# A conv-and-MLP decoder layer on one core: the gate row turned in DRAM at an earlier product and loaded later, and one quarter's squares run later

## The chip, the core and the metric

The kernel runs on one core of a Trainium2 chip. The metric is the device time of one execution in microseconds (us). A span is the time from the first to the last instruction of one profiled execution. TensorE multiplies (PE in the profile; PEld is its loading of weights), VectorE (DVE) and ScalarE (ACT) do the elementwise work, GpSimd (POOL) does some of it in the first half, and SyncE (SP) issues nearly all transfers, in the order of its program.

## The reference

One layer over 256 tokens of width 2048, in float32: a convolution mixer, then an MLP of width 8192. The last gate is a row of 2048 numbers that scales the MLP's output, column by column.

```python
mod = silu(c) @ mod_w + mod_b
sh1, sc1, g1, sh2, sc2, g2 = split(mod, 6)
h = rms_norm(x, norm1_g) * (1 + sc1) + sh1
x = x + (1 + g1) * conv_mixer(h)
h = rms_norm(x, norm2_g) * (1 + sc2) + sh2
u = square(relu(h @ mlp_w1))             # 256 x 8192
x = x + (1 + g2) * (u @ mlp_w2)          # 256 x 2048
```

## The kernel before

**Tiling.** The MLP's width of 8192 is cut into four quarters (numbered 0 to 3 in the code). A quarter has a first product (`h @ mlp_w1`, called `up`) and a second product (`u @ mlp_w2`, called `down`), which adds to the output `y`, kept in SBUF. Each product is a list of jobs. In quarters 1 to 3 some jobs are Strassen-like block products: the jobs called `seven` in the first product, `eight` in the second. The order of the jobs is written out by hand in two tables, `SEVEN_JOBS` (L75) and `LAST_JOBS` (L78). A number in parentheses there stands for a plain job of the first product, or for an `eight` job of the second. So the second product of a quarter runs `down 4`, `eight 1`, `down 6`, `eight 5`, `eight 7`, `eight 3`, `down 5` and so on.

**Weights.** A weight tile of 1 MB (`raw`, 128x2048) is loaded by SyncE into one of 7 buffers (`top_up`, L212). A job's weights are split in two halves of 128x1024 each: ScalarE writes the rounded part `hi` (L236), VectorE the rest `lo` (L240), each into one of 6 buffers. Three matmuls then take each pair: hi by hi, lo by hi and hi by lo (L310 to L312 in the plain jobs, L376 to L378 in `eight`, L484 to L486 in `seven`). In the block products VectorE first adds one raw tile to another (L336 in `seven`, L356 in `eight`). A buffer of `raw` comes free when the last split or sum that reads it is done, and the next load in SyncE's program may be waiting for it. So TensorE frees `hi` and `lo`, these free `raw`, and this starts loads.

**Activations between the products.** The first product leaves four blocks of 128x512 per token half. A block is transposed by VectorE in squares of 32 (L514), written to a DRAM tile `flat` (L515), and read back in another order (`turn_in`, eight transfers, L532) into two tiles `two`. `square` then runs on ScalarE: relu (L541), square (L543), rounded part (L251), and on VectorE the rest (L254). The results `u2` are the moving side of the second product. `read_block` does the read at once and leaves `square` to a task at the job number that it is given: tasks run while the splits of a job are put out. `block_out` (L1139) calls it for the last two blocks, numbered 2 and 3, from the first job of the second product on, whose number is `at`.

**The gate row.** The columns of `g2` are made by VectorE (L669, then a bias in L624), one per job here and there, as a 128x16 table in `modc`. The last column falls in the third quarter's second product. The table is then written to DRAM as one row of 2048 numbers, 4 bytes at a time (`gates`, L1497), and this row is read back into all 128 partitions as a tile of 1 MB (L1500, into `cond`, called `cb`). `cb` scales the last quarter's results, in `finish` (L446) and in `scale_y` (L1165).

**Order.** A scheduler puts the instructions of each engine in a row by priorities and by its own estimate of time; `issue_after` pins some of them behind others. At run time each engine works through its row in order, and waits on semaphores.

Of the kernel before, what the change touches and what calls it, by code (L numbers as in the profile page):

```python
# [15 lines left out]
P = 128  # L16
T = 256
D = 2048
KT = D // P
FF = 4 * D  # L20
QUARTERS = FF // D
# [57 lines left out]
EIGHT = (1, 2, 3)  # L79
# [8 lines left out]
def conv_block(ctx: ExitStack, tc: tile.TileContext, x, vec, dwq, c_row, mod_r, mod_t, mod_c, w_first, w_in, w_out, w1, w2, out):  # L88
    nc = tc.nc
# [41 lines left out]
    for i in range(2):  # L131
        p = ps.tile([P, 2, 2 * T], F32, name="mm", bufs=2)
        for n in range(2):
            at = 8 * i + 4 * n
            nc.tensor.matmul(p[:, n, :], ones[0:1, :], cond[0:1, at : at + 4, :], start=True, stop=True)
        nc.scalar.activation(cond[:, 8 * i : 8 * i + 8, :].rearrange("p k n -> p (k n)"), p.rearrange("p a b -> p (a b)"), AF.Silu)
    cb = cond.rearrange("p k n -> p (k n)")
    nc.scalar.activation(cz[:, :, 3], col("c", 0, KT), AF.Silu)
    state = {"used": 0}
# [388 lines left out]
    def turn_in(flat):  # L528
        halves = [two() for _ in range(2)]
        for h, s in enumerate(halves):  # L530
            for g in range(4):
                nc.sync.dma_start(  # L532
                    s[32 * g : 32 * g + 32].rearrange("p k (a t) -> p (k a) t", t=32),
                    flat[2 * h : 2 * h + 2, :, :, 32 * g : 32 * g + 32].rearrange("k a i t -> i (k a) t"),
                )
        return halves
# [49 lines left out]
    def mod_tile(at):  # L586
        w = take(("tile", at))
        j = TILES.index(at)
        for k in range(KT):
            g = k % 4  # L590
            state["row_end"] = nc.tensor.matmul(
                row_ps[0][32 * g : 32 * g + 32, j * P : (j + 1) * P], cz[:, k, 0:32], w[:, k, :], start=False, stop=False
            )
# [87 lines left out]
    def mods(keys):  # L681
        for key in keys:
            if key[0] == "mod":
                mod_chunk(*key[1:])
            elif key[0] == "tile":
                mod_tile(key[1])
            else:
                mod_col(key[1])
# [27 lines left out]
    def two():  # L716
        return tmp.tile([P, 2, T], F32, name="two", bufs=6)
# [53 lines left out]
    for job in jobs:  # L771
        n = quota.get(job, 0)
# [5 lines left out]
        if job[:2] in LATE_GATE:  # L778
            n = LATE_GATE[job[:2]][job[2]]
# [132 lines left out]
    for k in range(KT):  # L912
# [4 lines left out]
        if c == 0:  # L917
            n = two()
# [215 lines left out]
    def read_block(at, q, n, flat):  # L1134
        with tc.issue_after(state["load"].ins) if n > 2 else ExitStack():
            halves = turn_in(flat)
        at_job(at, square, q, n, halves)

    def block_out(at, q, n, sums):  # L1139
        flat = new_flat()  # L1140
        for t, _, p in sums:
            turn_out(flat, t, p)
        if n == 3:
            read_block(at + (2 if q in EIGHT else 1), q, 2, kept_of["flats"][0])
            read_block(at + {2: 4, 3: 4}.get(q, 1), q, n, flat)
        else:
            at_job(at + 1, read_block, at + 2, q, n, flat)

# [23 lines left out]
    chain, sums_of, kept_of, half_sums = {}, {}, {}, {}  # L1172
    squared = [None, None]

    for n, job in enumerate(jobs):
# [278 lines left out]
        elif kind == "up":  # L1454
            if job[1:] == (0, 0):
                state["gate_bias"] = x_pool.tile([P, KT], F32, name="gb")
                nc.vector.tensor_copy(state["gate_bias"], col("modb", G2 * KT, KT))
                for k2 in range(HALF):
                    modulate(k2, scaled(k2, r2), SH2, SC2, ps_two())
            if plain:  # L1460
                with urgent():
                    t2 = evac(p)
                    a = two()
                    nc.vector.tensor_tensor(t2, t2, spread(r2), op=ALU.mult)
                    for c in range(2):
                        at = 2 * i + c
                        nc.scalar.activation(t2[:, c, :], t2[:, c, :], AF.Relu, bias=shc[:, at : at + 1])
                    nc.vector.tensor_tensor(a, t2, t2, op=ALU.mult)
                u2[i] = mp.tile([P, 2, 2 * T], F32R, name="u2", bufs=HALF)
                split_act(u2[i], a)  # L1470
            elif i % 2 and job[1] in SEVEN:
                if i == 3 and job[1] in EIGHT[:-1]:
                    room["raw"] -= 1
                at_job(n + 1, block_out, n + 1, job[1], i // 2, sums.pop((kind, i // 2)))
                for k2 in range(2) if i == 7 and job[1] in EIGHT else ():
                    at_job(n + 1, make_half_sums, job[1], k2)
            elif i % 2:
                with urgent():
                    turn_block(job[1], i // 2, sums.pop((kind, i // 2)))
            mods(after[job])  # L1480
            if job[1] == 0:
                if i == 0:
                    turned = scratch.tile([KT, P, T], F32, name="turned")
                    y = xs.rearrange("p k t -> p (k t)").rearrange("p (b f) -> p b f", b=2)
                turn(i)
        else:
            with tc.issue_after(state["w_lo"]), tc.issue_after(state.get("drain", state["w_lo"])):
                mods(after[job])
            if job[1] == 0 and i in SUMS_AT:
                if i == SUMS_AT[0]:  # L1490
                    kept = scratch.tile([4, P, HALF, 2, P], F32, name="kept")
                with tc.issue_after(state["w_lo"]):
                    make_sums(SUMS_AT.index(i))
            if job == ("down", 2, 3):
                gates = scratch.tile([1, D], F32, name="gates")
                with tc.issue_after(state["load"].ins):
                    nc.sync.dma_start(gates[0].rearrange("(k p) -> p k", p=P), modc[:, G2 * KT : G2 * KT + KT])  # L1497
            if job == ("down", 2, 7):
                with tc.issue_after(state["load"].ins):
                    nc.sync.dma_start(cb, gates.to_broadcast([P, D]))  # L1500
            if job == ("down", QUARTERS - 1, 1):
                with tc.issue_after(state["load"].ins):
                    pieces[3] = fetch(3)
            if job == ("down", QUARTERS - 1, 3):
                with tc.issue_after(state["w_lo"]):
                    for t in range(2):
                        at = slice(1536, 2048)
                        scale_y(y[:, t, at], at, pieces[3][t])
            if i % 2 == 0:
                continue  # L1510
            for t, cs, p in sums.pop((kind, i // 2)):
                at = slice(512 * (i // 2) + cs.start, 512 * (i // 2) + cs.stop)
                s = y[:, t, at]
                if job[1] == 0:
                    nc.scalar.activation(s, p, AF.Copy)
                elif job[1] not in EIGHT:
                    state["drain"] = nc.vector.tensor_tensor(s, p, s, op=ALU.add).ins
                else:
                    end = finish if job[1] == QUARTERS - 1 else drain
                    if i in (1, 5):  # L1520
                        at_job(n + 1, end, i // 2, t, cs, p)
                    else:
                        end(i // 2, t, cs, p)
# [59 lines left out]
```

## Time and profile before

| what | value |
|---|---|
| time, median of 3 runs | 1077.24 us (1075.87 to 1087.63) |
| time of the profiled execution | 1076.28 us |
| its span | 1074.5 us |
| PE busy | 1052.1 us, 98% of the span |
| DVE busy | 908.9 us, 85% |
| ACT busy | 607.2 us, 57% |
| mean granted TensorE clock | 0.994 |
| fourth quarter's first product | about 896 to 985 us |
| second quarter's second product | about 643 to 729 us |

The time is 1.78 us above the span; that remainder lies around the first and the last instruction. A busy PE is not by itself a PE at its peak, but in the MLP the matmuls of 128x512 start every 0.23 us and overlap, and a longer step between two starts is time lost. The stage times in the table are read from TensorE's timeline.

### The profile page before, as it was taken

The page shows a single profiled execution, that of the slowest core. Times are in us where ns is not written, and L with a number is a line of the kernel's source. Part 1 is how long each engine was busy: PE and PEld are TensorE (multiplying, and loading weights), DVE is VectorE, ACT ScalarE, POOL GpSimd, SP SyncE. Part 2 cuts the span into 40 slices and gives each one's busy share as a digit, 9 for nine tenths or more (in the row PEclk, how much of TensorE's full clock was granted, in tenths as well). Part 3 has the DMA queues.
Part 4 walks back from the last instruction along what each step waited for, and adds up shares of the span by engine and source line. Part 5 has one row for each costly group of instructions (what it writes and reads, how often), then busy time and mean ns, then how long its engine had stood idle before and what let it go on. Part 6 is the DMA issues. An engine that isn't in the chain of part 4 may idle for free.

```text
span 1074.5 us, 15584 instructions
## 1 busy us (share of the span) xinstructions
PE 1052.1 (98%) x5844; PEld 868.6 (81%) x5844; DVE 908.9 (85%) x1176; ACT 607.2 (57%) x841; POOL 221.4 (21%) x153
## 2 busy tenths in 40 slices
PE   7999999999999999999999999999999999899998
PEld 3888886778699998888888888788888888688886
DVE  5777789988767889877889897999899899599996
ACT  4111298876875687444556576546566645456751
POOL 0000079989599261000000000000000000000001
PEclk8999999999999999999999999999999999999999
DMA  9999997996999978999986997793999792889853
GB/s 384 421 420 420 416 419 306 360 392 238 403 408 403 371 267 294 314 320 323 339 328 225 328 281 242 259 367 124 348 266 288 269 362 86 263 285 348 225 152 59
DMA packets 154334, 331.01 MB, mean 308 GB/s; under 512 B 88465, under 2 KB 114321, under 8 KB 119313
## 3 DMA queue, kind: packets, MB, share of 16 engines
q1 hardware_dynamic: 153248, 328.30, 83.8%
q0 software_dynamic: 864, 1.57, 1.1%
q8 instruction: 46, 0.75, 0.3%
q14 instruction: 30, 0.25, 0.1%
q10 hardware_dynamic: 146, 0.13, 0.0%
HBM read 313.71 MB, written 17.83 MB: 309 GB/s over the span
## 4 chain that ended last, share of the span: by engine, by line
PE 79%; DMA 12%; DVE 5%; ACT 2%; issue 1%; SPq 0%; ACTq 0%; DVEq 0%
PE mm L311 12%; PE mm L312 12%; PE mm L310 12%; DMA raw<-mod_c 9%; PE mm L268 6%; PE mm L269 3%; PE acc L265 3%; PE acc L264 3%; PE acc L266 3%; PE row L576 2%; PE mm L1090 2%; DMA raw<-w 2%; DVE lo L240 2%; PE acc L485 1%; PE acc L486 1%; PE acc L484 1%
## 5 line engine op out<-in xcount | busy, mean ns | idle before, releaser
L236 ACT ACTIVATE hi<-raw 128x1024 fp32r<-128x1024 f32 x374 | 383.4, 1054 | 261.6 <-PE mm L312 122.2
L240 DVE TENSOR_TENSOR lo<-raw,hi 128x1024 fp32r<-128x1024 f32 x313 | 370.6, 1217 | 60.4 <-ACT hi L236 59.9
L240 POOL TENSOR_TENSOR lo<-raw,hi 128x1024 fp32r<-128x1024 f32 x61 | 154.9, 2568 | 29.9 <-ACT hi L236 29.9
L669 DVE SCALAR_TENSOR_TENSOR raw<-raw,cond 128x2048 f32<-128x2048 f32 x50 | 117.7, 2355 | 27.7 <-DMA raw<-mod_c 27.7
L460 POOL DMA_DIRECT2D out<-two x6 | 5.4, 902 | 650.0 <-DVE two L458 638.9
L310 PE MATMUL mm<-hi,u 128*128 128x512 f32 x320 | 124.1, 389 | 0.7 <-ACT hi L236 0.7
L311 PE MATMUL mm<-lo,u 128*128 128x512 f32 x320 | 124.5, 389 | 0.0
L312 PE MATMUL mm<-hi,u 128*128 128x512 f32 x320 | 124.1, 389 | 0.0
L310 PE MATMUL mm<-hi,hl 128*128 128x512 f32 x288 | 112.6, 391 | 4.3 <-ACT hi L236 4.3
L311 PE MATMUL mm<-lo,hl 128*128 128x512 f32 x288 | 112.9, 392 | 0.8 <-DVE lo L240 0.8
L312 PE MATMUL mm<-hi,hl 128*128 128x512 f32 x288 | 112.5, 391 | 0.0
L969 DVE SCALAR_TENSOR_TENSOR acc<-u,v,acc 128x256 f32<-128x256 f32 x230 | 91.4, 477 | 0.0
L268 PE MATMUL mm<-hl,hi 128*128 128x512 f32 x224 | 80.0, 401 | 0.0
L310 PEld LDWEIGHTS mm<-hi,u 128*128 128x128 f32 x320 | 60.1, 188 | 13.5 <-ACT hi L236 1.1
L312 PEld LDWEIGHTS mm<-hi,u 128*128 128x128 f32 x320 | 60.1, 188 | 12.8 <-DVE u L254 0.4
L311 PEld LDWEIGHTS mm<-lo,u 128*128 128x128 f32 x320 | 60.1, 188 | 12.6
L310 PEld LDWEIGHTS mm<-hi,hl 128*128 128x128 f32 x288 | 54.4, 189 | 16.1 <-ACT hi L236 4.8
L873 PE MATMUL mm<-two,first 128*128 128x256 f32 x240 | 57.4, 394 | 8.4 <-ACT two L931 8.4
L311 PEld LDWEIGHTS mm<-lo,hl 128*128 128x128 f32 x288 | 54.4, 189 | 12.4 <-DVE lo L240 1.1
L312 PEld LDWEIGHTS mm<-hi,hl 128*128 128x128 f32 x288 | 54.5, 189 | 11.3
L265 PE MATMUL acc<-hl,hi 128*128 128x256 f32 x224 | 63.4, 283 | 0.0
L264 PE MATMUL acc<-hl,hi 128*128 128x256 f32 x224 | 63.4, 283 | 0.0
(381 smaller groups left out, 2067.1 us busy)
## 6 DMA issues: line engine op xcount, KB each, us to landing
raw<-w SPq DMA_DIRECT2D x128, 1024.0 KB, 7.9
raw<-mod_c SPq DMA_DIRECT2D x64, 1024.0 KB, 10.2
raw<-mod_r SPq DMA_DIRECT2D x28, 1024.0 KB, 9.2
raw<-w_in SPq DMA_DIRECT2D x16, 1024.0 KB, 10.4
raw<-w_out SPq DMA_DIRECT2D x16, 1024.0 KB, 8.5
first<-w_first SPq DMA_DIRECT2D x15, 1024.0 KB, 19.8
u<-kept SPq DMA_DIRECT2D x24, 512.0 KB, 8.4
flat<-two SPq DMA_DIRECT2D x30, 256.0 KB, 7.7
```

Source lines behind the costliest of these rows:

```text
L236: state["w_hi"] = nc.scalar.activation(hi, w[:, ks, :], AF.Copy).ins
L240: end = by.tensor_tensor(lo, w[:, ks, :], hi.bitcast(F32), op=ALU.subtract)
L264: nc.tensor.matmul(out_p, w, m[:, 0:T], start=begin, stop=False)
L265: nc.tensor.matmul(out_p, w, m[:, T : 2 * T], start=False, stop=False)
L266: state["mm_end"] = nc.tensor.matmul(out_p, lo[:, k % HALF, :], m[:, 0:T], start=False, stop=end)
L268: nc.tensor.matmul(p[:, c, :], hi[:, k % HALF, :], m, start=(k == 0), stop=(k == KT - 1))
L310: nc.tensor.matmul(p, p_hi, hi, start=begin, stop=False, skip_group_check=shared)
L311: nc.tensor.matmul(p, p_hi, lo, start=False, stop=False, skip_group_check=shared)
L312: nc.tensor.matmul(p, p_lo, hi, start=False, stop=end, skip_group_check=shared)
L669: end = nc.vector.scalar_tensor_tensor(w, w, 1.0, cb, op0=ALU.mult, op1=ALU.mult, accum_out=acc)
L873: step = nc.tensor.matmul(held[n][:, c, :], w[:, 2 * n + c, :], h, start=k == 0 and c == 0, stop=k == KT - 1, skip_group_check=True)
L969: end = nc.vector.scalar_tensor_tensor(out, s, w, acc, op0=ALU.mult, op1=ALU.add)
```

## The change

Two things are changed. First, in the second quarter (number 1) the squares of block 2 run at the task of job `at + 3` in place of `at + 2`, and those of block 3 at `at + 4` in place of `at + 1`. In the other two quarters the numbers stay what they were (2 and 4). Second, the write of the gate row to DRAM is put out at the job `down 1` of the third quarter in place of `down 3`, two jobs earlier in that table, and its read into all partitions at the plain job 3 of the fourth quarter's first product in place of the third quarter's last job.

```diff
@@ block_out
         if n == 3:
-            read_block(at + (2 if q in EIGHT else 1), q, 2, kept_of["flats"][0])
-            read_block(at + {2: 4, 3: 4}.get(q, 1), q, n, flat)
+            read_block(at + {1: 3, 2: 2, 3: 2}[q], q, 2, kept_of["flats"][0])
+            read_block(at + 4, q, n, flat)
@@ in the loop over the jobs, kind "up"
             mods(after[job])
+            if job == ("up", QUARTERS - 1, 3):
+                with tc.issue_after(state["load"].ins):
+                    nc.sync.dma_start(cb, gates.to_broadcast([P, D]))
@@ in the loop over the jobs, kind "down"
-            if job == ("down", 2, 3):
+            if job == ("down", 2, 1):
                 gates = scratch.tile([1, D], F32, name="gates")
                 with tc.issue_after(state["load"].ins):
                     nc.sync.dma_start(gates[0].rearrange("(k p) -> p k", p=P), modc[:, G2 * KT : G2 * KT + KT])
-            if job == ("down", 2, 7):
-                with tc.issue_after(state["load"].ins):
-                    nc.sync.dma_start(cb, gates.to_broadcast([P, D]))
```

In the new program the write of the gate row is L1500 and its read L1483.

ScalarE in the second quarter's second product, from the instruction behind the `L427` pair on; `two_6009` and `two_6010` are block 2, `two_6019` and `two_6020` block 3, `raw_5804`, `raw_5814` and `raw_5884` the weights of the `eight` jobs, `small` a PSUM bank that is copied out. Before:

```order
L541 ACTIVATE two_6019<-two_6019 128x512
L236 ACTIVATE hi_6158<-raw_5804 128x1024
L236 ACTIVATE hi_6162<-raw_5804 128x1024
L541 ACTIVATE two_6009<-two_6009 128x512
L541 ACTIVATE two_6010<-two_6010 128x512
L543 ACTIVATE two_6019<-two_6019 128x512
L1220 ACTIVATE rowsb_6138<-small_6140 128x512
L541 ACTIVATE two_6020<-two_6020 128x512
L543 ACTIVATE two_6009<-two_6009 128x512
L543 ACTIVATE two_6010<-two_6010 128x512
L251 ACTIVATE u2_6120<-two_6019 128x2x256
```

The same place on ScalarE with the change, from the same predecessor on:

```order
L236 ACTIVATE hi_6148<-raw_5804 128x1024
L236 ACTIVATE hi_6152<-raw_5804 128x1024
L1220 ACTIVATE rowsb_6128<-small_6130 128x512
L236 ACTIVATE hi_6206<-raw_5814 128x1024
L236 ACTIVATE hi_6210<-raw_5814 128x1024
L541 ACTIVATE two_6009<-two_6009 128x512
L541 ACTIVATE two_6010<-two_6010 128x512
L236 ACTIVATE hi_6239<-raw_5884 128x1024
L543 ACTIVATE two_6009<-two_6009 128x512
L543 ACTIVATE two_6010<-two_6010 128x512
L236 ACTIVATE hi_6243<-raw_5884 128x1024
L541 ACTIVATE two_6019<-two_6019 128x512
```

Block 3's relu stood first and now stands behind six splits; block 2's comes first, behind four splits. The second PSUM copy `q5<-row` (L1220), which TensorE needs, has 20 instructions ahead of it here before, and 16 now.

SyncE around the write of the gate row; `raw_7828` and what follows are 1 MB loads for the fourth quarter's first product. Before:

```order
L212 DMA raw_7828<-w1 128x2048
L212 DMA raw_7832<-w1 128x2048
L212 DMA raw_7846<-w1 128x2048
L212 DMA raw_7868<-w1 128x2048
L212 DMA raw_7878<-w1 128x2048
L1497 DMA gates_7944<-modc_116 128x16x1
```

The same place with the change:

```order
L212 DMA raw_7828<-w1 128x2048
L1500 DMA gates_7832<-modc_116 128x16x1
L212 DMA raw_7834<-w1 128x2048
L212 DMA raw_7848<-w1 128x2048
L212 DMA raw_7870<-w1 128x2048
L212 DMA raw_7880<-w1 128x2048
```

The write has moved ahead of four loads. The read of the row, on SyncE a little later before the change (`u2<-kept` loads sums for a block product, `out<-turned` copies the residual from DRAM to DRAM):

```order
L467 DMA out<-turned_4028 32x16x32 x2
L212 DMA raw_8077<-w1 128x2048
L1500 DMA cond_73<-gates_7944 128x2048
L212 DMA raw_8087<-w1 128x2048
L502 DMA u2_8089<-kept_4802 128x1024
```

And where it stands with the change, `flat` being the first block of the fourth quarter on its way to DRAM:

```order
L212 DMA raw_8236<-w1 128x2048
L212 DMA raw_8246<-w1 128x2048
L212 DMA raw_8281<-w1 128x2048
L212 DMA raw_8284<-w1 128x2048
L1483 DMA cond_73<-gates_7832 128x2048
L515 DMA flat_8361<-two_8362 128x4x128
L515 DMA flat_8361<-two_8365 128x4x128
```

It has moved behind seven more weight loads, four loads of sums and six residual copies, to a place right ahead of the first block's two writes. TensorE's order changes with it in one place: the 24 matmuls of job `seven 3` in the fourth quarter start ahead of those of plain job 3, as they do in the third quarter, in place of behind the first 12 of them.

## The prediction

> **What bounds the kernel now.** I read the page first, then compared stages that do the same work by windows, then followed the chain of waits, SyncE's timeline and the transfers at the place where two such stages differ. The page has the engines' shares and the chain by engine:
>
> ```profile
> span 1074.5 us, 15584 instructions
> PE 1052.1 (98%) x5844; PEld 868.6 (81%) x5844; DVE 908.9 (85%) x1176; ACT 607.2 (57%) x841; POOL 221.4 (21%) x153
> PE 79%; DMA 12%; DVE 5%; ACT 2%; issue 1%; SPq 0%; ACTq 0%; DVEq 0%
> ```
>
> TensorE is the bound: time can come only from places where its matmuls stand or go slowly. The DMA share of the chain lies mostly in the first half, which the change does not touch. So I look at the stages it does touch, each beside its twin in the next or the last quarter. Columns: window, its length, busy time and instructions of PE, PEld, DVE, ACT, POOL, granted clock, DMA share, GB/s.
>
> ```profile
> 643.50:740.58 97.08, 96.29 (x423) 78.76 (x421) 87.90 (x88) 54.94 (x64) 0.00 (x0) 1.00 0.69 246
> 811.20:907.04 95.84, 95.76 (x422) 78.84 (x421) 88.54 (x88) 53.97 (x63) 0.00 (x0) 1.00 0.69 248
> 740.58:773.12 32.54, 32.54 (x143) 26.94 (x144) 29.70 (x25) 18.58 (x19) 0.00 (x0) 1.00 0.96 347
> 907.04:946.98 39.94, 34.84 (x144) 27.79 (x144) 27.42 (x22) 19.48 (x20) 0.00 (x0) 0.96 0.84 258
> ```
>
> The first pair runs from the same matmul of the second product to the same matmul early in the next first product, in quarters 1 and 2 (named by the code's numbers); the second pair follows on, in quarters 2 and 3. With the same matmuls (a record or two is missing), quarter 1 is 97.08 − 95.84 = **1.24 us** longer than its twin, and the stretch at 907 is 39.94 − 32.54 = **7.40 us** longer than the one at 740. These two differences are what the edits can reach.
>
> The chain of waits at 907 (start, length, what):
>
> ```profile
> 908.15 4.90 DMA raw<-w
> 913.72 12.93 DMA raw<-w
> ...
> 927.84 1.24 DVE lo L240
> ...
> 929.91 0.43 PE mm L312
> ```
>
> A weight load issued at 913.72 takes 12.93 us where the one ahead of it took 4.90; its split, and so TensorE, wait for it. Then the matmuls step by 0.43 us, about half speed. The windows price both: PE stands 39.94 − 34.84 = 5.1 us in the stretch, and in its twin not at all; the other 7.40 − 5.1 = 2.3 us are the slow steps behind the pause, with the granted clock at 0.96 over the whole stretch.
>
> What stands in SyncE's row there:
>
> ```profile
> 908.15 0.33 SPq L212 DMA_DIRECT2D raw<-w  x1
> 908.53 0.43 SPq L1497 DMA_DIRECT2D gates<-modc  x1
> 909.00 4.62 SPq L467 DMA_DIRECT2D out<-turned  x2
> 913.72 4.04 SPq L212 DMA_DIRECT2D raw<-w  x1
> 923.15 0.33 SPq L1500 DMA_DIRECT2D cond<-gates  x1
> 923.59 0.37 SPq L212 DMA_DIRECT2D raw<-w  x1
> ```
>
> And the transfers from issue to landing (KB each, median us): the gate row's write, the residual's copies behind it, the same copies in quarter 2, an undisturbed 1 MB load, and the load issued at 923.59 behind `cond`:
>
> ```profile
> gates<-modc SPq DMA_DIRECT2D x1, 8.0 KB, 14.6
> out<-turned SPq DMA_DIRECT2D x1, 64.0 KB, 15.4
> out<-turned SPq DMA_DIRECT2D x2, 64.0 KB, 4.8
> raw<-mod_c SPq DMA_DIRECT2D x1, 1024.0 KB, 6.1
> raw<-w SPq DMA_DIRECT2D x1, 1024.0 KB, 8.3
> ```
>
> The write of 8 KB takes 14.6 us, and what is queued behind it waits: the copies take 15.4 instead of 4.8, the load 12.9 instead of 6.1. I put the hold on the queue at 12.9 − 6.1 = 6.8 us at least, and 15.4 − 4.8 = 10.6 at most. The Trainium skill, page "DMA: Bandwidth & Descriptors", section "Anatomy of one DMA — SWDGE (gpsimd) path", gives a transfer as about 2.0 us and its bytes at 436 GB/s. By that 8 KB would be an estimated 2.02 us; the trace has 14.6. The fit is for transfers from GpSimd, and it has no term for pieces of 4 bytes.
>
> **The gate row's write, two jobs sooner.** One issue is removed at 908.53 and put ahead of four weight loads (the two raw tiles of the first `seven` sum, then two plain ones), behind the load that the trace has at 874.77. Removed at 908: the hold, so the load of 913.72 lands in about 6 us, by 920, as in quarter 2, where TensorE does not pause. The pause and the slow steps go together, and the stretch becomes its twin: **−7.40 us**. Nothing is next late there in the twin: its PE is busy through all of the 32.54 us.
>
> Added at 875: the same hold, on four loads. SyncE's row, DVE's last step of the table, the two `seven` sums that need the first of these loads, and the window between the last landing and the next issue:
>
> ```profile
> 874.77 33.71 SPq L212 DMA_DIRECT2D raw<-w  x5
> 874.71 0.15 DVE L624 TENSOR_TENSOR modc<-modc,gb 128x1 f32<-128x1 f32 x1
> 900.23 2.28 DVE L336 TENSOR_TENSOR raw<-raw 128x2048 f32<-128x2048 f32 x1
> 903.57 2.28 DVE L336 TENSOR_TENSOR raw<-raw 128x2048 f32<-128x2048 f32 x1
> 889.90:908.10 18.20, 18.12 (x81) 14.68 (x80) 18.17 (x14) 9.02 (x10) 0.00 (x0) 1.00 0.00 1
> ```
>
> The table is ready at 874.86, so SyncE's wait for it, which it had already at 874.77, costs nothing new. The transfers then stand idle for 18.2 us, from 889.90 to 908.10: all loads are down, and seven buffers are full. A hold of 6.8 to 10.6 us is taken out of this idle time. The sum at 900.23 has its two tiles by about 895, the last plain tile comes by 900.5, ahead of its split, which stands behind the second sum's end at 905.85. Cost 0, with some 5 us to spare for either; if the hold were over 14 us the cover is gone, and each microsecond more would be one of TensorE's.
>
> **The gate row's read, half a product later.** One issue of 1 MB moves from 923.15 to about 950: past seven weight loads, four loads of kept sums and six residual copies, to just ahead of the first block's write to `flat` of quarter 3. What it is moved past gains; the 7.40 holds that already. Its readers are in the last quarter's second product, after 985, and it lands near 960. Its source, the row in DRAM, is down 50 us before: no wait. What is queued behind it is `flat`, then two more loads. The write of `flat` in quarters 2 and 3, ScalarE's relu that waits for its way back, and the one matmul group that this costs something in quarter 3:
>
> ```profile
> flat<-two SPq DMA_DIRECT2D x2, 256.0 KB, 6.1
> flat<-two SPq DMA_DIRECT2D x2, 256.0 KB, 8.2
> 804.87 0.63 ACT L541 ACTIVATE two<-two 128x512 f32<-128x512 f32 x1 [1.77 <-DMA two<-flat]
> 980.20 0.63 ACT L541 ACTIVATE two<-two 128x512 f32<-128x512 f32 x1 [3.25 <-DMA two<-flat]
> PEld mm L312 <- DVE u L254: 0.4, 1, 0.4
> ```
>
> The price of 1 MB in a full queue: the load of 913.72 landed at 926.65, that of 923.59 at 923.59 + 8.3 = 931.9, and between them came `cond` and this load: 5.3 / 2 = 2.6 us each. Without the jam of 907 the flat would land as in quarter 2, in 6.1 us, and with `cond` ahead of it in about 8.7, where it took 8.2 before. So this end of quarter 3 may be 0.5 us later than it was, and its relu already waits, with a trace of it at TensorE (0.4). Bounds: 0, if the 0.5 stays in ScalarE's slack, and 2.6, if the whole MB shows. I take **+0.5**, nearest to the row of 8.2.
>
> **The squares of quarter 1.** Nothing is added or removed; eight relus, squares and splits on ScalarE move one to three jobs on. The DVE sum ahead of the place, the relu that waits, two splits, the copy out of PSUM, and the matmul and the weight load that wait for the second of these splits and for the copy:
>
> ```profile
> 655.68 2.28 DVE L356 TENSOR_TENSOR raw<-raw 128x2048 f32<-128x2048 f32 x1
> 660.82 0.63 ACT L541 ACTIVATE two<-two 128x512 f32<-128x512 f32 x1 [5.27 <-DMA two<-flat]
> 672.31 1.99 ACT L236 ACTIVATE hi<-raw 128x1024 fp32r<-128x1024 f32 x2
> 674.20 0.58 ACT L1220 ACTIVATE q<-row 128x512 f32<-128x512 f32 x1
> 674.35 0.50 PE L310 MATMUL mm<-hi,u 128*128 128x512 f32 x1 [0.71 <-ACT hi L236]
> 674.83 0.19 PEld L376 LDWEIGHTS row<-hi,raw 128*128 128x128 f32 x1 [0.30 <-ACT q L1220]
> ```
>
> ScalarE stood 5.27 us for block 3's read, with splits queued behind that needed nothing but the sum that ended at 655.68 + 2.28 = 657.96. With the change they start there, 3.5 us sooner than behind the relu's end at 661.45. I replayed its row by these durations (about 0.97 for a split, 0.5 for each of the others when one follows the other): the second pair waits for DVE's next sum until about 663.9, the split that TensorE waited for ends near 672.3 instead of 674.30, and the copy near 673.4 instead of 674.78. TensorE wants the split from 674.35 − 0.71 = 673.64 on and the copy one matmul (0.23 us) later, so the copy has some 0.4 us to spare by these rows; block 3 is squared by ScalarE and VectorE before its own matmuls, by the replay with 0.6 us to spare. The stall of 0.71 and the 0.30 behind it go; I take the whole difference of the twins, **−1.24 us**. Bounds: 0, if the stall only moves, and 1.24, since the twin has hardly a pause left (95.76 of 95.84 us busy).
>
> **The sum.** −7.40 − 1.24 + 0.5 = −8.1 us. The profiled execution took 1076.28 us (span 1074.5 and 1.78 around it), 0.96 below the median of 1077.24. So 1076.28 − 8.1 = **1068.2 us**, with a span of 1066.4.
>
> **The rivals.** *The read shows in full.* The whole 2.6 us reach TensorE at the end of quarter 3, where a relu already waits 3.25: 1068.2 + 2.1 = 1070.3. For it, the 0.4 at L312; against it, that 3.25 us of ScalarE's waiting cost TensorE only that. Chance 0.13.
>
> *Quarter 1 stalls all the same.* The slack of 0.4 us comes out of a replay of some twenty instructions, each with an error of a few hundredths: 1068.2 + 1.24 = 1069.4. Chance 0.12.
>
> *The row is not what held the load.* If the write were short by itself and only landed late in a crowd, moving it removes nothing: the 7.40 stay, and 1076.28 − 1.24 = 1075.0. The fit of the Trainium skill, page "DMA: Bandwidth & Descriptors", would have it so. Against it: at 908 the queue was empty after 18 idle us, so there was no crowd but the row itself, one load and the copies. Chance 0.06.
>
> *Slower: the row holds the loads of the first sums past 900.23.* Placed among five full loads, the 4-byte pieces might be served far more slowly than in an empty queue. It begins to cost at a hold of 14 us; TensorE would then pause as at 927 and pay about 2.3 us of slow steps besides. The gain is gone at a hold of 14 + 8.1 − 2.3 = 20 us, and at one of 33 us the time is 1068.2 + 19 + 2.3 = 1089.5. The trace has 10.6 at most. Chance 0.04.
>
> **How the numbers follow.** The forecast, 1068.2, is 1067.7 where the read costs nothing, and 0.4 less in a run as short as the shortest (1076.28 − 1075.87); it is 1069.2 where the 0.96 between execution and median comes on top. Its own range is 1067.3 to 1069.3, its chance 0.60. Something better than the twins, which no row shows, gets 0.05. The range reaches from 1066.4, the own range less about the spread once more, to 1071.3, which takes in the first two rivals with the spread of 0.96. One per cent, about what a measurement here can tell from no change, is 1066.5 below and 1088.0 above: all of the first three rivals and nearly all of the forecast are within it, though it says 0.84% faster. Faster by over 1%: the 0.05, and 0.05 of the forecast's low end. Slower by over 1%: the last rival.
>
> **What would show it.** Right: the stretch of the fourth quarter from the same matmul as 907.04 is 32.5 us long, with a clock of 1.00, and no load there takes over 9 us; the row's write stands at 875, its four loads land by 901, and the idle time of transfers shrinks from 18 us to about 10. Quarter 1's window is 95.8 us, and the relu's 5.27 is gone or short. The relu at 980 waits 3 to 4 us. Wrong: a pause before the first `seven` sum at 900; a load of 12 us still in the stretch at 907; a pause of TensorE at the end of quarter 3 of over 1 us; a stall of 0.7 at the copy out of PSUM.

## The result and the profile after

| | before | changed |
|---|---|---|
| median, 9 runs each | 1076.48 us (1075.32 to 1087.63) | 1068.8 us (1067.68 to 1069.55) |
| ratio | | 0.9918, 95% interval 0.9892 to 0.9943 |
| profiled execution, its span | 1076.28, 1074.5 us | 1069.55, 1067.8 us |

The forecast was 1068.2 us, 9.0 us or 0.84% below the median known then (1077.24). The medians of the nine runs fell by 7.68 us or 0.71%, and the changed kernel's stands 0.6 us above the forecast. One run of before, at 1087.63 us, lies 11 us above its median: with it the ratio of the means is 0.9918, without it 0.9929. The page of the changed kernel, engines' shares and chain as before:

```profile
span 1067.8 us, 15591 instructions
PE 1050.8 (98%) x5844; PEld 868.2 (81%) x5844; DVE 911.9 (85%) x1176; ACT 607.9 (57%) x841; POOL 220.2 (21%) x153
PE 80%; DMA 10%; DVE 5%; ACT 2%; issue 2%; SPq 0%; ACTq 0%; DVEq 0%
```

The windows of the changed kernel, cut at the same matmuls as in the prediction (quarter 1's second product; the stretch that held the jam, up to the first `acc<-u` matmul of its next `seven` job; and from there to the end of the span):

```profile
643.56:739.40 95.84, 95.76 (x423) 78.84 (x421) 88.46 (x88) 54.03 (x63) 0.00 (x0) 1.00 0.69 247
905.95:938.63 32.68, 32.68 (x143) 26.87 (x144) 27.60 (x22) 19.71 (x20) 0.00 (x0) 1.00 0.87 298
938.63:1067.80 129.17, 123.45 (x541) 101.00 (x539) 109.22 (x118) 69.12 (x83) 5.42 (x6) 0.99 0.72 210
```

The last of these in the kernel before:

```profile
946.98:1074.50 127.52, 122.83 (x541) 101.11 (x539) 109.11 (x118) 68.89 (x83) 5.42 (x6) 0.99 0.72 208
```

Quarter 1 went from 97.08 to 95.84 us (−1.24), the stretch from 39.94 to 32.68 (−7.26) with a clock of 1.00, and the last stage grew from 127.52 to 129.17 (+1.65). With 0.06 more ahead of quarter 1 and 0.09 more between the two (905.95 − 739.40 against 907.04 − 740.58), that is −6.70, the difference of the two spans. The profiled execution is one of the two longest of the nine, 0.75 us above their median. In what follows "the jam" is the stretch's late load, and "the last stage" the third window.

SyncE in the changed kernel, the landing of the first load behind the write (KB, us), the first sum that needs it, and the window of idle transfers behind the loads:

```profile
875.64 0.55 SPq L1500 DMA_DIRECT2D gates<-modc  x1
876.28 31.11 SPq L212 DMA_DIRECT2D raw<-w  x4
907.44 1.24 SPq L467 DMA_DIRECT2D out<-turned  x2
909.87 0.33 SPq L212 DMA_DIRECT2D raw<-w  x1
raw<-w SPq DMA_DIRECT2D x1, 1024.0 KB, 17.8
899.14 2.28 DVE L336 TENSOR_TENSOR raw<-raw 128x2048 f32<-128x2048 f32 x1
899.01:907.06 8.05, 7.97 (x36) 6.28 (x35) 8.02 (x6) 3.77 (x5) 0.00 (x0) 1.00 0.00 0
```

The hold is still there: a load of 17.8 us. But it lands at 876.28 + 17.8 = 894.1, 5 us ahead of its sum, and what the hold takes is idle time of the transfers, of which 8 us are left out of 18. Of the four loads behind the write, three go out there; the fourth waits for a buffer and goes out at 907.06, as it did at 908.15 before.

ScalarE in quarter 1, block 2's relus, the split that TensorE had stalled for, and the copy out of PSUM:

```profile
665.79 1.14 ACT L541 ACTIVATE two<-two 128x512 f32<-128x512 f32 x2
671.33 1.04 ACT L236 ACTIVATE hi<-raw 128x1024 fp32r<-128x1024 f32 x1
672.80 0.57 ACT L1220 ACTIVATE q<-row 128x512 f32<-128x512 f32 x1
```

No relu waits for a transfer there any more; the split ends at 672.37 and the copy at 673.37, and TensorE's matmuls start every 0.23 us through the place.

The end of quarter 3's first product: the landing of the first flat, the relu behind it, and two matmuls that wait:

```profile
flat<-two SPq DMA_DIRECT2D x2, 256.0 KB, 9.7
973.47 0.63 ACT L541 ACTIVATE two<-two 128x512 f32<-128x512 f32 x1 [4.13 <-DMA two<-flat]
977.61 0.50 PE L310 MATMUL mm<-hi,u 128*128 128x512 f32 x1 [0.74 <-ACT u L251]
978.56 0.50 PE L376 MATMUL small<-hi,u 128*128 128x512 f32 x1 [0.22 <-ACT hi L236]
```

This is the one place that got worse. Flat takes 9.7 us to land where it took 8.2, the relu waits 4.13 where it waited 3.25, and TensorE loses 1.8 us, where it lost 0.2 before: from 976.49 on, the steps from one matmul's start to the next include 1.12, 0.61 and 0.55 us among the usual 0.23.

### The profile page after: what moved, and what is told of

Its sections match the earlier page's. It is cut to its first block, busy times and chain, and to the rows that moved or that the text cites. A ratio compares the mean times of both kernels' runs of the same rounds, so it can differ in the third digit from the quotient of the medians.

```text
span 1067.8 us, 15591 instructions
## 1 busy us (share of the span) xinstructions
PE 1050.8 (98%) x5844; PEld 868.2 (81%) x5844; DVE 911.9 (85%) x1176; ACT 607.9 (57%) x841; POOL 220.2 (21%) x153
## 4 chain that ended last, share of the span: by engine, by line
PE 80%; DMA 10%; DVE 5%; ACT 2%; issue 2%; SPq 0%; ACTq 0%; DVEq 0%
PE mm L312 12%; PE mm L310 12%; PE mm L311 12%; DMA raw<-mod_c 7%; PE mm L268 6%; PE mm L269 3%; PE acc L265 3%; PE acc L264 3%; PE acc L266 3%; PE mm L1090 2%; PE row L576 2%; DVE raw L669 1%; DVE lo L240 1%; PE acc L485 1%; PE acc L486 1%
## 5 line engine op out<-in xcount | busy, mean ns | idle before, releaser
L266 PE MATMUL acc<-hl,lo 128*128 128x256 f32 x224 | 63.4, 283 | 0.0
L312 PEld LDWEIGHTS mm<-hi,hl 128*128 128x128 f32 x288 | 54.1, 188 | 11.3
L311 PEld LDWEIGHTS mm<-lo,hl 128*128 128x128 f32 x288 | 54.1, 188 | 11.3
## 6 DMA issues: line engine op xcount, KB each, us to landing
raw<-w_in SPq DMA_DIRECT2D x16, 1024.0 KB, 10.6
```

Source lines behind the costliest of these rows:

```text
L266: state["mm_end"] = nc.tensor.matmul(out_p, lo[:, k % HALF, :], m[:, 0:T], start=False, stop=end)
L311: nc.tensor.matmul(p, p_hi, lo, start=False, stop=False, skip_group_check=shared)
L312: nc.tensor.matmul(p, p_lo, hi, start=False, stop=end, skip_group_check=shared)
```

## The experiments

Three questions were open. Is it the write of the gate row that makes the jam, and by its pieces of 4 bytes? What does the read ahead of the first flat cost? And do the squares give their 1.2 us by themselves?

**The squares alone.** Kernel before, with this:

```diff
-            read_block(at + (2 if q in EIGHT else 1), q, 2, kept_of["flats"][0])
-            read_block(at + {2: 4, 3: 4}.get(q, 1), q, n, flat)
+            read_block(at + {1: 3, 2: 2, 3: 2}[q], q, 2, kept_of["flats"][0])
+            read_block(at + 4, q, n, flat)
```

> Only the squares of quarter 1 are moved; the gate row is written and read where it was before. If the stall of 0.71 and the wait behind it came from block 3's relu standing at the head of ScalarE's row: quarter 1's window falls from 97.08 us to 95.8, the jam at 907 stays with its load of about 12.9 us (stretch 39.9), the time is about 1.2 us below before. If the stall had another cause that only the sooner write removes: the window stays at 97.1 and the time does not move.

1076.31 us against 1076.84 of before beside it (ratio 0.9997, 0.9988 to 1.0007). Its windows:

```profile
643.75:739.60 95.85, 95.76 (x423) 78.85 (x421) 88.46 (x88) 54.08 (x63) 0.00 (x0) 1.00 0.70 250
906.20:946.93 40.73, 35.88 (x143) 28.31 (x144) 27.51 (x22) 19.48 (x20) 0.00 (x0) 0.92 0.84 252
946.93:1075.30 128.37, 123.44 (x541) 101.04 (x539) 109.14 (x118) 69.06 (x83) 5.42 (x6) 0.99 0.72 207
```

The window falls as expected, to 95.85, so moving the squares takes the stall away without the sooner write. But only 0.5 us arrive, within the noise. In this profile the jam is 0.8 us longer than in the first one of before and the last stage 0.85. Whether that belongs to the order was asked again below.

**The write alone, two jobs sooner.** Kernel before, with this:

```diff
-            if job == ("down", 2, 3):
+            if job == ("down", 2, 1):
```

> Only the write of the gate row is put two jobs sooner; its read stays in quarter 2's last job, the squares stay as before. If the write alone held the load of 913.72: the stretch at 907 falls from 39.9 us to about 32.7, with no load over 10 us in it, and, since no 1 MB read then stands ahead of the first flat of quarter 3, the stage behind it keeps its 127.5 us: some 7.3 us below before. If the read behind it was half of the jam (1 MB in the same queue): the stretch stays above 35 us. If the longer end of the changed kernel (129.2 us) has nothing to do with the read: 129.2 here too, and only 5.6 us below before.

1068.79 us (ratio 0.9928, 0.9912 to 0.9945), 8.05 below before. Jam stretch and last stage:

```profile
906.54:939.19 32.65, 32.65 (x143) 26.87 (x144) 27.37 (x22) 19.60 (x20) 0.00 (x0) 1.00 0.94 325
939.19:1066.60 127.41, 122.70 (x541) 101.11 (x539) 109.29 (x119) 68.96 (x83) 5.42 (x6) 1.00 0.71 206
```

The write alone makes the jam: without it TensorE is busy through all of the stretch, though the read now stands right in it (issued at 908.07) and one load there still takes 10.8 us, more than the 10 expected at most. One edit of one number has the whole gain of the change.

**The read alone, half a product later.** Kernel before, with the read taken from `("down", 2, 7)` to `("up", QUARTERS - 1, 3)` as in the change, and nothing else.

> Only the read of the gate row is put half a product later; the write stays at 908, the squares as before. If the write is the jam: the stretch at 907 stays between 37 and 40 us, and the first flat of quarter 3 waits for the read's 1 MB as in the changed kernel (9.5 us to landing, 8.1 before), so the stage behind is 129.2 us instead of 127.5: 0 to 1.7 us above before. If the read was the jam: the stretch falls to about 33 us, and the time by 5 us or more.

1079.3 us (ratio 1.0022, 1.0013 to 1.0032): 2.5 us above before, more than either theory had. The stretch, what TensorE waited for in it, and the transfer in the chain:

```profile
906.78:949.65 42.87, 34.90 (x143) 28.21 (x144) 27.60 (x22) 19.48 (x20) 0.00 (x0) 0.92 0.85 257
PE row L484 <- DMA u<-kept: 8.0, 1, 8.0
917.92 13.21 DMA u<-kept
```

The jam stays, as the write's theory says, and it is another operand that is late. With the read gone from the job, the scheduler puts the 24 matmuls of `seven 3` (`row<-u`) ahead of those of plain job 3, as in the change. Their kept sums were issued at 917.92, behind the write, and landed at 931.13; TensorE stood 8.0 us in this one wait, where it stood 5.1 in the whole stretch before. So moving the read is harmful until the write is out of the way. The last stage, 127.65, did not grow by 1.7. The run also answers a rival that the prediction does not name: in before, SyncE itself stood 5.3 us at the read (up to 923.15), waiting for the row to land, and could issue nothing. But the late load of 913.72 had been issued ahead of that wait, and here, where no read stands, the same load (issued at 913.55) takes 13.8 us.

**The changed kernel without the late read.** The change, with the read put back to quarter 2's last job:

```diff
-            if job == ("up", QUARTERS - 1, 3):
-                with tc.issue_after(state["load"].ins):
-                    nc.sync.dma_start(cb, gates.to_broadcast([P, D]))
...
+            if job == ("down", 2, 7):
+                with tc.issue_after(state["load"].ins):
+                    nc.sync.dma_start(cb, gates.to_broadcast([P, D]))
```

> The changed kernel with the read of the gate row put back to quarter 2's last job: write sooner and squares later stay. If the read ahead of the first flat costs the 1.65 us by which the last stage grew: quarter 1's window 95.8 us, the stretch at 907 about 32.7, the last stage 127.5, so 8.4 us below before and 1.7 us below the changed kernel. If the last stage grew because the loads ahead of the flat now run in a fuller queue: it stays at 129 us, and the time is that of the changed kernel.

1067.78 us (ratio 0.9919, 0.9905 to 0.9934). The last stage, and the flat's landing:

```profile
938.67:1065.90 127.23, 122.56 (x541) 101.20 (x539) 109.46 (x119) 69.54 (x83) 5.42 (x6) 1.00 0.71 206
flat<-two SPq DMA_DIRECT2D x2, 256.0 KB, 7.4
```

The last stage is at 127.2 and the time 1.0 us below the changed kernel's 1068.8: less than the 1.65 of the one profile, in the direction of the read's theory. Against the write alone, which differs from it by the squares, it is 1.0 us faster: there the squares' gain arrives.

**Wider pieces at the old place.** Kernel before, with the write in pieces of 64 bytes, which puts the numbers in another order (the output's columns are scaled by one another's gates):

```diff
-                    nc.sync.dma_start(gates[0].rearrange("(k p) -> p k", p=P), modc[:, G2 * KT : G2 * KT + KT])
+                    nc.sync.dma_start(gates[0].rearrange("(p k) -> p k", p=P), modc[:, G2 * KT : G2 * KT + KT])
```

> The kernel before, with one thing changed: the write of the gate row, at its old place at 908, is in 128 pieces of 64 bytes instead of 2048 of 4, so the numbers stand in the row in another order and the output's columns are scaled by one another's gates. If the pieces of 4 bytes hold the queue: the write lands in 5 us or less, the load issued at 913.7 lands in 7 us or less, the stretch at 907 is 33 us instead of 39.9, the last stage stays at 127.3 to 128.4, and the time is some 7 us below before with nothing moved. If the write's place or any write of the table at that point is the cause: the load still takes 12 to 13 us and the time stays.

1068.8 us against 1077.05 (ratio 0.9926, 0.9911 to 0.994). The landing of the write and of the load behind it, and the stretch:

```profile
gates<-modc SPq DMA_DIRECT2D x1, 8.0 KB, 4.7
raw<-w SPq DMA_DIRECT2D x1, 1024.0 KB, 7.0
907.35:939.99 32.64, 32.64 (x143) 26.87 (x144) 27.37 (x22) 19.60 (x20) 0.00 (x0) 1.00 0.94 326
```

At the same place in the queue, with the same 8 KB, the write takes 4.7 us instead of 14.6, the load behind it 7.0 instead of 12.9, and the jam is gone. That load is also issued sooner, since SyncE puts out the two copies ahead of it in 1.24 us instead of 4.62: counted from the stretch's start it lands after 10.9 us instead of 19.6, so the hold was 8.7 us. It was the 2048 pieces of 4 bytes, not the place and not the bytes in all. Number and size of the pieces changed together here, and no run parts them: the two residual copies behind the write are 1024 pieces of 128 bytes, and with wide pieces ahead of them they land in 4.6 and 5.3 us. The last stage came out at 128.71, above the 127.3 to 128.4 expected; the table below takes that up.

**The row written twice.** The changed kernel, with a second write just ahead of the first, to a row of its own that nobody reads:

```diff
+                    again = scratch.tile([1, D], F32, name="again")
+                    nc.sync.dma_start(again[0].rearrange("(k p) -> p k", p=P), modc[:, G2 * KT : G2 * KT + KT])
```

> The changed kernel with the row written twice, one after the other, to two rows in DRAM, at the sooner place. In the changed kernel the first load behind the write took 17.8 us and landed at 894.1, 4 to 5 us ahead of its sum at 899.1. If the hold grows with the number of pieces, by about 10 us for a write: that load lands at 904, the sum starts near 904 instead of 899.1, TensorE pauses for up to 4 us some 2 us later and pays one or two spells at half clock (1.7 us lost in each 3.4): 1 to 7 us above the changed kernel. If the two writes overlap in the queue, or if the margin is wider than I read it: the same time as the changed kernel, within 0.5 us.

1071.11 us (ratio 0.9948, 0.9932 to 0.9965), 2.5 above the changed kernel run beside it (1068.65). The second write's landing, the first sum, two matmuls, and the window between the stretches (166.55 in the changed kernel):

```profile
gates<-modc SPq DMA_DIRECT2D x1, 8.0 KB, 22.8
901.78 2.29 DVE L336 TENSOR_TENSOR raw<-raw 128x2048 f32<-128x2048 f32 x1 [2.61 <-DMA raw<-w]
905.27 0.50 PE L484 MATMUL acc<-hi,u 128*128 128x512 f32 x1 [0.82 <-ACT hi L236]
908.60 0.50 PE L485 MATMUL acc<-lo,u 128*128 128x512 f32 x1 [1.65 <-DVE lo L240]
739.34:908.60 169.26, 166.79 (x733) 137.17 (x733) 154.72 (x151) 101.51 (x117) 0.00 (x0) 1.00 0.85 270
```

The load of the first sum now lands at 901.75, where it landed at 894.1, and the last of the group at 906.73, where it landed at 899.0: the second write holds the queue for about 7.7 us. It uses up the 5 us to spare, and the sum starts 2.6 us later. TensorE pauses twice, for 0.82 and 1.65 us, and the window is 2.7 us longer, with no half clock.

**The read in the idle time.** The changed kernel, with the read put out at the `eight` job 4 of quarter 2, between the two jobs of the gate row; on SyncE it then stands two loads behind the write:

```diff
             mm_eight(bank[i], *job[1:])
+            if job == ("eight", 2, 4):
+                with tc.issue_after(state["load"].ins):
+                    nc.sync.dma_start(cb, gates.to_broadcast([P, D]))
...
-            if job == ("up", QUARTERS - 1, 3):
-                with tc.issue_after(state["load"].ins):
-                    nc.sync.dma_start(cb, gates.to_broadcast([P, D]))
```

> The changed kernel with the read of the gate row put between the loads of 885.8 and 886.3, where the queue is empty soon after, in place of ahead of the first flat. If all that the late read cost was its 1 MB ahead of the flat: the flat of quarter 3 lands 7 to 8 us after issue (9.5 in the changed kernel), the last stage is 127.3 us instead of 129.2, and the time is 1.5 to 2 us below the changed kernel, as with the read in quarter 2's last job. If SyncE's wait for the row there (until about 894) makes the load behind it late: TensorE pauses at 907 to 912 and the gain goes again.

1067.73 us (1067.44 to 1067.84; ratio 0.9914, 0.9899 to 0.9929), the shortest of all, though not apart from the kernel with the read in quarter 2's last job. Its last stage:

```profile
938.40:1065.70 127.30, 122.57 (x541) 101.16 (x539) 108.81 (x118) 69.14 (x83) 5.41 (x6) 0.99 0.72 205
```

The read was issued at 890.13, after SyncE had waited 7.5 us for the row, and was down at 899.2; TensorE waited for no load (the window between the stretches is 166.55 us, as in the changed kernel).

**The changed kernel again**, as it is.

> The changed kernel as it is, beside the other three on one chip: 7.5 to 8.5 us below before; the last stage 1.3 to 2 us longer than in the kernel with the read in the idle time, by both theories; if its profile shows the last stage at 127.5 us, the 129.2 of the first profile was chance.

1068.65 us (ratio 0.9924, 0.991 to 0.9939). The last stage and the flat's landing:

```profile
938.96:1066.40 127.44, 122.80 (x541) 101.09 (x539) 109.11 (x118) 69.02 (x83) 5.42 (x6) 1.00 0.73 213
flat<-two SPq DMA_DIRECT2D x2, 256.0 KB, 8.5
```

So the 129.17 of the first profile was partly chance: with the same program the flat landed 1.2 us sooner here, and TensorE lost next to nothing. The expected 1.3 to 2 us against the read in the idle time are 0.14 in these profiles and 0.9 in the medians.

**Three more profiles** were made for that scatter: of before, of the squares alone, and of the changed kernel.

> The kernel before, for a second profile of the jam and of the last stage. In its first profile the pause of 4.73 us was followed by 3.4 us at half clock and the last stage took 127.5 us, with the first flat landing 11.3 us after the stage's start; with the squares alone moved, the same pause was followed by 6.8 us at half clock, and the last stage took 128.4 us, with the flat at 12.1. If both are scatter from run to run, this profile may show either (one or two spells of 3.4 us; a last stage of 127.3 to 129), with quarter 1 at 97.1 us. If they belong to the order, it shows one spell and 127.5 us again.

> The squares of quarter 1 alone moved, for a second profile: quarter 1 at 95.8 us by every theory. If its lost 0.7 us was scatter: one spell of half clock as likely as two, and a last stage anywhere from 127.3 to 129 us. If it belongs to the order: two spells and 128.4 us again.

> The changed kernel, for a third profile of the last stage, which took 129.2 us in the first and 127.4 in the second: quarter 1 at 95.8 us and the stretch at 907 at 32.6 by every theory. If the length of the last stage is set by when the first flat lands: under 11.5 us after the stage's start goes with less than 0.4 us lost, over 12 us with over 1 us.

The stretch in before's second profile:

```profile
906.74:947.55 40.81, 36.09 (x144) 28.72 (x145) 27.50 (x22) 19.46 (x20) 0.00 (x0) 0.92 0.85 262
```

The squares alone, second profile, stretch and last stage:

```profile
906.32:946.77 40.45, 35.81 (x143) 28.57 (x144) 27.31 (x22) 19.35 (x20) 0.00 (x0) 0.92 0.84 259
946.77:1074.00 127.23, 122.56 (x541) 101.20 (x539) 109.22 (x119) 69.36 (x83) 5.41 (x6) 1.00 0.71 207
```

The changed kernel, third profile, last stage and flat:

```profile
938.60:1067.40 128.80, 123.39 (x541) 101.01 (x539) 109.20 (x118) 69.12 (x83) 5.42 (x6) 0.99 0.73 211
flat<-two SPq DMA_DIRECT2D x2, 256.0 KB, 9.4
```

Before's own jam is 39.94 in one profile and 40.81 in the other, and the squares alone have a last stage of 128.37 and of 127.23. So the 0.7 us that the squares alone seemed to lose lie within the scatter of single profiles, on a kernel whose runs lie 3.6 us apart (1075.23 to 1078.85 in that set). All profiles together, by when the first flat landed after the last stage's start:

| kernel | read ahead of the flat | first flat landed after | last stage |
|---|---|---|---|
| before, second profile | no | 10.4 us | 127.25 us |
| read in quarter 2's last job | no | 10.6 | 127.23 |
| squares alone, second | no | 10.7 | 127.23 |
| read in the idle time | no | 11.0 | 127.30 |
| write alone | no | 11.2 | 127.41 |
| before, first | no | 11.3 | 127.52 |
| row written twice | yes | 11.7 | 128.06 |
| read alone | yes | 11.8 | 127.65 |
| changed, second | yes | 11.9 | 127.44 |
| squares alone, first | no | 12.1 | 128.37 |
| wider pieces | no | 12.2 | 128.71 |
| changed, third | yes | 12.7 | 128.80 |
| changed, first | yes | 13.0 | 129.17 |

The flat is what the last stage's length goes by. Counting TensorE's steps above 0.27 us, each profile loses time in this stage at one place only, 36 to 50 us after the stage's start: 0 us where the stage took 127.2 or 127.3, 1.8 where it took 129.17. The relu ahead of that place starts 20.8 to 22.3 us after the first flat's landing in all thirteen. Up to about 11.3 us the flat costs TensorE 0.3 us or less; from there each microsecond costs roughly one, with scatter. The read ahead of it moves the mean from 11.2 (eight profiles) to 12.2 us (five), over the edge. But two of the eight without it are over the edge as well. What delayed the flat in those two isn't settled: the loads queued ahead of it landed late too, and nothing was tried on it.

## Why the prediction was right

**The jam, −7.40.** Right in place, cause and size: −7.26 in the profiles. That the write's pieces hold the queue was argued from the rows of before; the write alone and the wider pieces show it. The hold was put at 6.8 to 10.6 us; by the times of landing it measures 7.7 for the second of two writes and 8.7 at the old place, inside the bounds. One thing under the term was not seen: what a pause costs in slow steps differs from run to run, and the one profile of before had the smaller price. With its second profile the term would have been 8.3. The rival that the row was not the cause falls.

**The hold at 875, cost 0.** Right, and the margin too: the loads were put at about 895 and 900.5, and landed at 894.1 and 899.0. Only their number was off: three loads stood behind the write at this place, not four, the fourth being the one of 908.15. The slower rival named a hold of 14 us as the point where it begins to cost. Two writes hold the queue for about 16.6 us: the first takes 8.9 (the group's last load lands at 899.0 instead of 891.2, with the stage 1.1 us earlier), the second 7.7. That is 2.6 us over the point, and the window grew by 2.7, at the place and with the wait that the rival named. Its further price of half-speed steps did not appear behind these two pauses of 0.82 and 1.65 us. The changed kernel stays clear of it by 5 us, less than one more such write.

**The squares, −1.24.** Right: 97.08 to 95.84, the replay's split at 672.3 measured 672.37 and its copy at 673.4 measured 673.37. The term itself scatters: the five profiles with the old order have 96.46 to 97.42 in that window (mean 96.9), those with the new one 95.83 to 95.85. By the medians it is 1.0 us where the write is moved as well, and lost in the noise where it isn't. The rival of a stall all the same falls.

**The read, +0.5.** Right in sign and in what it rests on, too small in size: about 0.95 us by the medians (1068.8 and 1068.65 against 1067.78 and 1067.73), between 0.1 and 1.9 in single profiles. The forecast had the flat land in 8.7 us, and that came out: 8.3 to 9.7 in the four profiles with the late read and without the jam, mean 8.9. But neither of its two terms did. "Without the jam of 907 the flat would land as in quarter 2, in 6.1 us": without jam and without late read it landed in 7.4 to 9.0 us (write alone, read in the last job, wider pieces, read in the idle time), mean 8.1. And the read's 1 MB added 0.9 us, not 2.6. That the two errors cancel is luck. What the term lacked is the edge: behind some 11.3 us from the stage's start, the flat's delay is TensorE's. So this place cost 1.8, 0.2 and 1.6 us in the three profiles of the changed kernel. The sign of being wrong that the prediction named, a pause of over 1 us there, did not come as one pause (the longest wait is 0.74), but in two of the three the waits together cost more than that. The upper bound of 2.6 held, and the rival that the read shows in full, at 1070.3, was not reached.

**The sum.** −7.40 − 1.24 + 0.5 stands against −7.26 − 1.24 + 1.65 in the one profile, and against −7.7 in the medians of the first nine runs and −8.4 in those of the second set (1077.05 to 1068.65). The forecast came as near as it did because two errors have opposite signs: the jam's price was too small by 0.5 to 0.9 us (three further profiles of the same jam have 40.45 to 40.81 for its 39.94), the read's by about 0.5. That too is luck.

## What to carry to other kernels

Look at the pieces of a small transfer, their number and size, and not at its bytes alone, before placing it: 8 KB in 2048 pieces held back the loads behind it by about 8 us. Put such a write where the transfers are idle anyway, and look for what else in its neighbourhood is placed by it (here a scheduler's order of matmuls), since moving the one without the other can cost time. And a term read from a single pair of profiled stages carries the scatter of both: a second profile of the kernel before would have shown 0.9 us of it.

## What was not expected of the hardware

The clock after a pause. In before's first profile the granted clock was halved for about 3.4 us, in its second for twice as long, after pauses of nearly the same length (steps of 4.73 and 4.55 us). Windows of 1 us, the granted clock being the third number from the right; first profile:

```profile
928.00:929.00 1.00, 0.35 (x1) 0.04 (x1) 1.00 (x2) 0.75 (x1) 0.00 (x0) 0.94 0.99 418
929.00:930.00 1.00, 0.88 (x2) 0.79 (x3) 1.00 (x2) 0.00 (x0) 0.00 (x0) 0.50 1.05 442
...
932.00:933.00 1.00, 1.00 (x6) 0.75 (x4) 0.00 (x0) 0.00 (x0) 0.00 (x0) 0.86 1.03 391
```

Second profile:

```profile
927.00:928.00 1.00, 0.59 (x1) 0.20 (x1) 0.61 (x1) 1.00 (x2) 0.00 (x0) 0.76 1.01 426
928.00:929.00 1.00, 0.45 (x2) 0.34 (x2) 1.00 (x2) 0.30 (x1) 0.00 (x0) 0.50 0.99 418
...
934.00:935.00 1.00, 1.00 (x5) 0.82 (x4) 0.15 (x1) 0.82 (x1) 0.00 (x0) 0.82 1.04 435
```

A row's clock says how much of it was at half: 0.94 is 0.12 us, 0.86 is 0.28, and with the three rows at 0.50 between them that is 3.4 us. The second profile has 0.48 + 6 + 0.36 = 6.8 us. The squares alone have about 6.8 in both profiles. The Trainium skill, page "TensorE: Matmul & The Clock Gate", Part 1, says that the clock is set from windows of 3413 ns that run freely, and drops after an idle one; the trace agrees with the length, one or two of them, and with a start that differs from run to run. Why there is a second one is not shown. The restart does not tell them apart: in all four profiles of this jam its first steps are 1.26 and 0.59 us. What differs is where the half clock begins. In the first profile that is at 928.9, 1.0 us behind the first matmul after the pause (927.86). In the four profiles with 6.8 us it is from 2.7 us ahead of that matmul to 0.1 us behind it: 927.5 against 927.41 in before's second, 925.9 against 927.01 and 926.4 against 926.99 with the squares alone, 928.6 against 931.27 with the read alone.

The price of small pieces. At the old place 2048 pieces of 4 bytes took 14.3 to 15.3 us to land, 128 pieces of 64 bytes with the same 8 KB took 4.7. The Trainium skill, page "DMA: Bandwidth & Descriptors", "Rules for kernel authors", says that a last dimension that isn't contiguous is lowered to one descriptor per element; the trace agrees, with 2078 packets under 512 bytes from 912 to 914. Shared out over the 1920 pieces more, the 10 us more are about 5 ns each, an estimate from these two times that takes the number to be the cause. But they are not spent in sending the pieces. Before's packets, its transfers in this and the next 2 us, and the latter with wide pieces (the last two numbers are the share of time in which the DMA engines were busy, and GB/s):

```profile
DMA packets 2097, 0.17 MB, mean 86 GB/s; under 512 B 2078, under 2 KB 2078, under 8 KB 2078
912.00:914.00 2.00, 2.00 (x10) 1.66 (x9) 1.20 (x2) 0.85 (x1) 0.00 (x0) 1.00 0.87 86
914.00:916.00 2.00, 2.00 (x10) 1.65 (x10) 1.76 (x2) 2.00 (x3) 0.00 (x0) 1.00 0.00 1
914.00:916.00 2.00, 2.00 (x11) 1.65 (x10) 1.40 (x2) 2.00 (x3) 0.00 (x0) 1.00 1.01 407
```

All pieces start within 2 us. Then the transfers stand, with two copies and a load of 1 MB issued and waiting, and up to 922 they move 18 to 71 GB/s, where wide pieces leave 407. What is waited for in that time, no run shows.
